# Attention values of a pair of heads in one group, and the end stage's loads spread out, in a two-layer hybrid decoder trunk on one Trainium2 core

## The chip, the core and the metric

The kernel runs on one core of a Trainium2 chip. The metric is the device time of one execution in microseconds (us), taken as the median of several. A profile of one further execution shows what each engine did: PE is the matmul engine (PEld its weight loads, which overlap with it), DVE the vector engine, ACT the scalar engine, POOL the general engine, and SP the queue that issues nearly all transfers. Each engine works through its own instructions in a fixed order; an instruction that has to wait holds up all that stand behind it on its engine.

## What is computed

Two layers over 512 tokens of width 1024. In each layer four branches read the same input; each result is gated, projected, and merged, and then an output projection, a residual and a layer norm follow. Branch B, causal attention with eight heads, is the one that changes here:

```python
def one_block(args):                       # one block of 128 queries, i = 0..3
    q_blk, i = args
    s = jnp.einsum('bqhd,bkhd->bhqk', q_blk, k).astype(jnp.float32) * scale
    s = jnp.where(key_idx[None, :] <= q_idx[:, None], s, MASK_VALUE)
    pr = jax.nn.softmax(s, axis=-1).astype(v.dtype)
    return jnp.einsum('bhqk,bkhd->bqhd', pr, v)
...
merged = jnp.sum(gates * proj, axis=2)     # over the four branches
out = merged @ w_out[l]
x = _layer_norm(DEEPNORM_ALPHA * x + out, ln_g[l], ln_b[l])
```

The other branches are a recurrent one (RWKV, 64x64 states), a convolution of width 31 with a layer norm, and a cross-attention into 256 memory tokens.

## The kernel before

**Who sets the order.** The kernel is written as many Python generators ("tasks") beside one stream of items. A planner (`Plan`, lines 67 to 196) keeps a modelled clock for each engine and, while the program is recorded, always steps the task that is due first; where no task is due, the stream goes on. The stream is the large projections: weights arrive through SP into two raw buffers (`weights`, line 430), are split into a high and a low part by ACT and DVE, and each product of 512 columns is made of three matmuls (`mm3`, line 461). What the planner decides is the fixed order in which each engine's instructions stand in the program; the chip does not reorder them. A task that yields "small" waits until other tasks of small matrices are due too (at most `GATHER` = 1500 ns of modelled time), so that matmuls that use half of the PE array stand together. The planner charges itself some time for each change between whole-array and half-array matmuls (`shape`, line 110).

**The attention branch.** The eight heads are taken as four pairs `hh`. For each pair `pair` (line 1460) takes one PSUM bank `mo` for the result and starts eight tasks `mla_block` (line 1477), for the query blocks i = 0 to 3 and the two heads h, at most three of them under way at a time. A block makes its scores `ms` on PE (128 queries by 128(i+1) keys, and the causal mask by one more matmul); DVE takes the maximum `nmm`; ACT the exponential `mP` with its sum; DVE divides; PE transposes the probabilities in pieces of 128x128 into `mt`; ACT copies them from PSUM to SBUF, `mPT` (lines 1502 to 1509). When the four blocks of i = 0, 1 are copied, six matmuls multiply them with the values `vtok` into `mo`; when the four of i = 2, 3 are, fourteen more follow (lines 1516 to 1520). These use 64 of the 128 columns of the array: one head goes to the upper half of `mo`'s partitions, the other to the lower. Each such float32 matmul shows as two records in the profile. After the second group `mo` is copied out (line 1526), and after the fourth pair the branch's pool is closed and the recurrent branch may begin.

The probabilities lie in a ring of four buffers with the tag `mPT`. A pair uses six of them: one for each head's blocks 0 and 1, and one each for blocks 2 and 3 of each head. So a copy reuses the buffer that was taken four before it, and must wait until the matmuls have read that.

**The merge.** `turn` (line 1537) decides when the gated result of a branch may be split into its high and low part (ACT and DVE, in `fin`, line 1548): when six of the eight merge steps of the branch ahead of it have been made. The order of the branches is cross-attention (3), attention (1), convolution (2), recurrent (0).

**The end stage.** When the recurrent branch is done, `start` (line 1641) opens a pool and issues the loads of the residual `z` in one go: eight of 128x512 in the first layer, sixteen of 128x256 in the second, and in the second also eight rows of layer-norm factors (`affine`, line 1651), four for the residual and four for the last norm. They go through SP's queue like the weights. A task `residual` then scales `z`, from the time when the last load it needs has landed by the planner's clock.

Of the kernel before, what the change touches and what calls it, by code (L numbers as in the profile page):

```python
# [265 lines left out]
def trunk_kernel(ctx: ExitStack, tc: tile.TileContext, A, out, dbg=None):  # L266
    nc = tc.nc
    plan = Plan(tc.keep_in_program_order)
    V, S, G = Engine(plan, nc.vector, "DVE"), Engine(plan, nc.scalar, "ACT"), Engine(plan, nc.gpsimd, "POOL")

    def MM(o, lhsT, rhs, start, stop, four=False):
        n = 1
        for d in rhs.shape[1:]:
            n *= d
        k, m = lhsT.shape[0], lhsT.shape[-1]
        plan.shape(64 if k <= 64 else 128, 64 if m <= 64 else 128)
        if max(k, m) <= 64:
            c = max(0.42 * n + 1.0, 29.0) if four else max(0.83 * n + 12.0, 59.0)
        elif rhs.dtype != F32 or n < 16:
            c = max(0.4167 * n + 13.0, 109.0) * (2 if rhs.dtype == F32 else 1)  # L280
        elif m <= 64:
            c = 0.83 * n + 3.0
        else:
            c = 1.667 * n + 5.0
        plan.op("PE", c, _names(o), _names(lhsT, rhs))
        plan.keep(nc.tensor.matmul(o, lhsT, rhs, start=start, stop=stop))  # L286
# [6 lines left out]
    def DMA(o, i, name=None):  # L293
        n = 512
        for d in o.shape[1:]:
            n *= d
        plan.dma(n, [name] if name else _names(o), _names(i))
        plan.keep(nc.sync.dma_start(o, i))
# [12 lines left out]
    pg = Space(plan, None, 0)  # L311
# [14 lines left out]
    def u(name, cols=512, dt=F32, p=128):  # L326
        return up.tile([p, cols], dt, tag="u", name=name)
# [217 lines left out]
    def close_phase():  # L545
        phase[0].close()
# [48 lines left out]
    def layer_items(l):  # L595
        items = []
        L = {}
        t_ = f"_{l}"
# [121 lines left out]
        def rwkv_unit(j0, hf, rkv):  # L720
# [485 lines left out]
        def xhead(h, q):  # L1206
# [3 lines left out]
            for tp in range(2):  # L1210
# [10 lines left out]
                yield  # L1221
            PT = []
            for mb in range(2):
# [31 lines left out]
        def m(name, cols, tag, bufs, p=128, dt=F32):  # L1255
            return L["mp"].tile([p, cols], dt, tag=tag, name=name, bufs=bufs)
# [101 lines left out]
        ymla = []  # L1358
# [101 lines left out]
        def pair(hh, qT, kT, there):  # L1460
            yield lambda: L["turn"] == hh and len(there) == 8
            mo, = yield from pg.take([128, 512], f"mo{hh}" + t_)
            plan.t = max(plan.t, *(plan.done[x][0] for x in there + [f"qTpe{hh}1" + t_]))
            yield
            left = [2]
            for i in range(4):
                if i % 2 == 0:
                    two, done = {}, []
                for h in range(2):
                    while L["jobs"] == 3:  # L1470
                        yield lambda: L["jobs"] < 3
                    L["jobs"] += 1
                    plan.spawn(mla_block(hh, h, i, (qT[h], kT[h]), mo, two, done, left))
                    yield
            L["turn"] += 1

        def mla_block(hh, h, i, T, mo, two, done, left):
# [24 lines left out]
            if i > 1:  # L1502
                PT = m("mPT" + q, 512, "mPT", 4)
            else:
                if h not in two:
                    two[h] = m("mPT" + q, 512, "mPT", 4)
                PT = two[h][:, 128 * i:]
            PT = two[h, i] = PT[:, 0:n]
            S.copy(PT, ps)
            pg.free()  # L1510
            L["jobs"] -= 1
            done.append(q)
            if len(done) < 4:
                return
            yield "small"
            for b in (i - i % 2, i - i % 2 + 1):
                for kb in range(b + 1):
                    for half in range(2):
                        MM(mo[HALF[half], 128 * b:128 * b + 128], vtok[kb][:, 128 * hh + 64 * half:128 * hh + 64 * half + 64],
                           two[half, b][:, 128 * kb:128 * kb + 128], start=kb == 0, stop=kb == b)  # L1520
            left[0] -= 1
            if left[0] == 0:
                L["pairs"] += 1
                yield
                yo = u(f"mo{hh}" + t_)
                S.copy(yo, mo)
                pg.free()
                ymla.append(yo)
                if len(ymla) == 4:
                    close_phase()  # L1530
                    L["mla"] = True


        merged = [None] * 8
        added = [0] * 4

        def turn(n):
            return n == 3 or added[{1: 3, 2: 1, 0: 2}[n]] >= 6

        def gate_items(n, base, name, ready, ys, res, op):  # L1540
            for i in range(4):
# [89 lines left out]
        E = {}  # L1631

        def end_items():
# [5 lines left out]
                return xs[zw * i // 512][:, zw * i % 512:zw * i % 512 + zw]  # L1639

            def start(get):
                yield lambda: "rwkv" in L
                E["ep"] = open_phase(f"ep{l}")
                ep = E["ep"]
                last = l + 1 == LAYERS
                E["z"] = [[ep.tile([128, zw], F32, tag=f"z{tb}{i}", name=f"z{tb}{i}" + t_) for i in range(zn)] for tb in range(4)]
                for tb in range(4):
                    for i in range(zn):
                        DMA(E["z"][tb][i], TOK[l][:, tb, zw * i:zw * i + zw])

                def affine(ll):
                    res = []
                    for n in ("ln_g", "ln_b"):
                        for i in range(2):
                            b = ep.tile([128, 512], F32, tag=f"{n}{i}{ll}", name=f"{n}{i}_{ll}" + t_)
                            DMA(b, A[n][ll, 512 * i:512 * i + 512].unsqueeze(0).to_broadcast([128, 512]))
                            res.append(b)
                    return res

                E["y"] = [0] * 4  # L1660
                if l:
                    ab = affine(l - 1)

                    def residual():
                        for i in range(zn):
                            for tb in range(4):
                                z, g, b = E["z"][tb][i], cut(ab[:2], i), cut(ab[2:], i)
                                if tb == 0:
                                    V.tensor_scalar(out=b, in0=b, scalar1=4.0 * ALPHA, scalar2=None, op0=ALU.mult)
                                V.scalar_tensor_tensor(out=z, in0=z, scalar=4.0 * ALPHA, in1=g, op0=ALU.mult, op1=ALU.mult)  # L1670
                                V.tensor_tensor(out=z, in0=z, in1=b, op=ALU.add)
                                E["y"][tb] += 1
                                yield "slack" if i else None
                    plan.spawn(residual(), plan.done[ab[3].tensor.name][0])
                else:
                    def residual():
                        for i in range(zn):
                            for tb in range(4):
                                z = E["z"][tb][i]
                                S.activation(z, z, AF.Copy, scale=4.0 * ALPHA)  # L1680
                                E["y"][tb] += 1
                                yield
                    plan.spawn(residual(), plan.done[E["z"][3][-1].tensor.name][0])
                if last:
                    E["ab"] = affine(l)

            def ahead(get):
                if l + 1 < LAYERS:
# [339 lines left out]
```

## Time and profile before

| | |
|---|---|
| three timed runs | 1508.65, 1511.56, 1513.46 us; median 1511.56 us |
| the profiled execution | 1509.62 us, of which the profile's span is 1507.8 us |
| PE busy | 1475.7 us, 98% of the span |
| DVE, ACT, POOL busy | 1072.6, 688.1, 134.3 us |
| granted TensorE clock, mean | 0.998 |
| attention branch on PE, first to last value matmul | 133.0 to 229.4 us in the first layer, 907.2 to 984.4 us in the second |
| end stage's loads issued by SP | 617.7 to 631.2 us in the first layer, 1377.9 to 1390.5 us in the second |

The profile has a page with busy times, a table of instruction groups and the chain of work that ended last; the trace behind it can be asked for the waits of each engine, for the instructions of a stretch in order of time (the timeline: start in us, duration in us, engine, line, operation, tiles written <- read, shape, count, and in brackets the idle time before it and what ended it), for one tile, and for busy times in windows of time. Buffer numbers are left out of tile names. Line 235 and 286 are helpers through which every instruction of an engine goes, so the tile names tell the stages apart. The end of a matmul is modelled; the distance between the starts of two is what PE needs for the first.

### The profile page before, as it was taken

The numbers are of one execution on the slowest core, as the hardware profiler recorded it, in microseconds if no ns is written. First come the engines' busy times: TensorE is split into PE (matmuls) and PEld (weight loads), VectorE is DVE, ScalarE is ACT, GpSimd is POOL, SyncE is SP. The second block draws the span as 40 slices with busy tenths as digits, with TensorE's granted clock in tenths as the row PEclk, the third lists the DMA queues.
The fourth block names the chain that finished last, engine by engine and source line by source line (L and its number), as shares of the span: only waits on it lengthen the run. The fifth ranks groups of instructions, "written<-read, shape, count | busy, mean of one in ns | idle before, by whom it ended". The sixth has DMA issues, their size and how long they took to land.

```text
span 1507.8 us, 29728 instructions
## 1 busy us (share of the span) xinstructions
PE 1475.7 (98%) x11896; PEld 1237.5 (82%) x11896; DVE 1072.6 (71%) x2231; ACT 688.1 (46%) x1507; POOL 134.3 (9%) x329
## 2 busy tenths in 40 slices
PE   8998999999999999999999999999999999999997
PEld 8887788888888888888999877888887888888886
DVE  5787998765758576555554889997866586757847
ACT  5544654345254454444255546533444354444432
POOL 0000000020403021000010000000030202020002
PEclk9999999999999999999999999999999999999999
DMA  6334333223232322433343242432232323234331
GB/s 212 119 115 98 105 100 98 96 77 95 62 86 81 95 88 81 140 98 120 121 144 114 83 126 68 121 109 93 82 98 69 94 74 94 65 104 142 126 119 63
DMA packets 89018, 153.54 MB, mean 102 GB/s; under 512 B 41008, under 2 KB 47152, under 8 KB 88880
## 3 DMA queue, kind: packets, MB, share of 16 engines
q1 hardware_dynamic: 88880, 151.65, 33.9%
q8 instruction: 93, 1.52, 0.4%
q14 instruction: 45, 0.37, 0.1%
HBM read 134.32 MB, written 5.77 MB: 93 GB/s over the span
## 4 chain that ended last, share of the span: by engine, by line
PE 91%; DVE 4%; DMA 2%; ACT 2%; issue 1%; SPq 0%; POOL 0%; ACTq 0%; DVEq 0%; POOLq 0%
PE ps_m L286 23%; PE po L286 12%; PE ps_xg L286 3%; PE ps_cg L286 3%; PE ps_rg L286 3%; PE ps_k L286 3%; PE ps_mg L286 3%; PE ps_v L286 3%; PE ps_r L286 3%; PE ps_val L286 3%; PE ms L286 2%; PE pz L286 2%; PE ps_glu L286 2%; PE ps_xq L286 2%; PE pl L286 2%; PE x L286 2%
## 5 line engine op out<-in xcount | busy, mean ns | idle before, releaser
L235 DVE SCALAR_TENSOR_TENSOR cacc<-hpad,prm,cacc 128x512 f32<-128x512 f32 x240 | 178.8, 747 | 3.3
L235 ACT ACTIVATE tm<-ps_m,prm 128x512 f32<-128x512 f32 x64 | 44.1, 689 | 141.2 <-PE ps_m L286 141.1
L235 DVE SCALAR_TENSOR_TENSOR mt<-tm,po 128x512 f32<-128x512 f32 x48 | 32.9, 686 | 71.2 <-PE po L286 69.0
L235 POOL TENSOR_TENSOR ZT<-ZT,tmpW 64x14 f32<-64x14 f32 (+6 forms) x112 | 42.7, 382 | 8.8
L235 ACT ACTIVATE mP<-ms,nmm 128x512 f32<-128x512 f32 (+3 forms) x64 | 33.7, 528 | 18.2 <-DVE nmm L235 17.4
L235 POOL TENSOR_TENSOR tmpW<-ZT,W 64x14 f32<-64x14 f32 (+6 forms) x112 | 39.3, 351 | 8.1
L235 POOL TENSOR_SCALAR ZT<-W 64x256 f32<-64x256 f32 x8 | 4.2, 524 | 383.8 <-DMA W<-scr 383.8
L235 ACT COPY mPT<-mt 128x512 f32<-128x512 f32 (+3 forms) x64 | 26.7, 428 | 22.2 <-PE mt L291 17.0
L235 DVE TENSOR_TENSOR merged<-merged,mt 128x512 f32<-128x512 f32 x48 | 33.5, 697 | 1.7
L235 POOL MEMSET D<- 128x8 f32 x8 | 1.1, 135 | 346.6 <-PE ms L286 327.1
L235 DVE TENSOR_REDUCE nmm<-ms 128x1 f32<-128x512 f32 (+3 forms) x64 | 29.9, 483 | 0.5
L291 PE MATMUL mt<-cst,mP 128*128 128x128 f32 x160 | 27.1, 277 | 2.4 <-DVE mP L235 2.3
L235 DVE TENSOR_SCALAR mP<-mP,smm 128x512 f32<-128x512 f32 (+3 forms) x64 | 24.8, 387 | 2.3
L235 DVE SCALAR_TENSOR_TENSOR merged<-tm,po 128x512 f32<-128x512 f32 x16 | 11.0, 687 | 20.8 <-PE po L286 19.1
L235 POOL TENSOR_SCALAR lrs<-lmv 128x1 f32<-128x1 f32 x8 | 2.5, 315 | 258.4 <-DVE lmv L235 256.7
L291 PEld LDWEIGHTS mt<-cst,mP 128*128 128x128 f32 x160 | 18.6, 141 | 8.0 <-ACT mo L235 2.2
L235 ACT ACTIVATE z<-z,lnb,lrs 128x256 f32<-128x256 f32 (+1 forms) x16 | 9.6, 648 | 31.1 <-DVE lnb L235 31.1
L235 ACT ACTIVATE yb<-yb,mr,gr 128x64 f32<-128x64 f32 x64 | 22.1, 428 | 2.7 <-DVE mr L235 2.7
L286 PE MATMUL ms<-kTl,qT 96*128 96x512 f32 (+3 forms) x64 | 22.3, 348 | 0.0
L286 PE MATMUL mo<-mPT,v 128*64 128x128 f32 x320 | 21.4, 278 | 0.5 <-ACT mPT L235 0.5
L235 POOL TENSOR_SCALAR gr<-gm 128x8 f32<-128x8 f32 x8 | 1.6, 198 | 215.5 <-DVE gm L235 215.5
L286 PEld LDWEIGHTS mo<-mPT,v 128*64 128x64 f32 x320 | 17.3, 136 | 4.0 <-issue 2.9
(3536 smaller groups left out, 5344.5 us busy)
## 6 DMA issues: line engine op xcount, KB each, us to landing
w<-in_w_ch_dram SPq DMA_DIRECT2D x146, 512.0 KB, 3.7
w<-in_w_o_dram SPq DMA_DIRECT2D x32, 512.0 KB, 3.7
w<-in_w_out_dram SPq DMA_DIRECT2D x16, 512.0 KB, 3.8
w<-in_w_lat_dram SPq DMA_DIRECT2D x16, 336.0 KB, 3.2
w<-in_w_mk_dram SPq DMA_DIRECT2D x8, 512.0 KB, 3.5
w<-in_w_mv_dram SPq DMA_DIRECT2D x8, 512.0 KB, 3.4
w<-in_w_qk_dram SPq DMA_DIRECT2D x8, 320.0 KB, 3.1
x<-in_xT_dram SPq DMA_DIRECT2D x8, 256.0 KB, 5.7
```

The lines of the kernel that those rows point to most:

```text
L235: return self.plan.keep(f(*a, **k))
L286: plan.keep(nc.tensor.matmul(o, lhsT, rhs, start=start, stop=stop))
L291: plan.keep(nc.tensor.transpose(o, i, ident))
```

## The change

1. All eight blocks of a pair are multiplied with the values in one group of twenty matmuls, when the last is copied (`len(done) < 8`); `left` goes.
2. The ring of four buffers goes. Each head has two buffers of 384 columns for its blocks 0 and 1 (tag `mPT0`, `mPT1`), and one of 896 columns for its blocks 2 and 3 (`mPW0`, `mPW1`). Before a pair takes these, the planner waits until the group of the pair before it (for the wide ones), or of two pairs before it (for the narrow ones), has been recorded.
3. `turn` asks for eight merge steps of the branch ahead in place of six.
4. `start` only starts a task `opening`, which issues the end stage's loads step by step: 3 us of planner time after the loads of each 128 tokens, 2 us after each row of factors.

```diff
-            left = [2]
+            two, done = {}, []
             for i in range(4):
-                if i % 2 == 0:
-                    two, done = {}, []
                 for h in range(2):
...
-            if i > 1:
-                PT = m("mPT" + q, 512, "mPT", 4)
-            else:
-                if h not in two:
-                    two[h] = m("mPT" + q, 512, "mPT", 4)
-                PT = two[h][:, 128 * i:]
-            PT = two[h, i] = PT[:, 0:n]
-            S.copy(PT, ps)
+            if (h, i // 2) not in two:
+                if L["pairs"] < hh - 1 + i // 2:
+                    yield lambda: L["pairs"] >= hh - 1 + i // 2
+                two[h, i // 2] = m("mPT" + q, 896, f"mPW{h}", 1) if i > 1 else m("mPT" + q, 384, f"mPT{h}", 2)
+            e = (0, 128, 0, 384)[i]
+            S.copy(two[h, i // 2][:, e:e + n], ps)
             pg.free()
             L["jobs"] -= 1
             done.append(q)
-            if len(done) < 4:
+            if len(done) < 8:
                 return
             yield "small"
-            for b in (i - i % 2, i - i % 2 + 1):
+            for b in range(4):
                 for kb in range(b + 1):
                     for half in range(2):
+                        e = (0, 128, 0, 384)[b] + 128 * kb
                         MM(mo[HALF[half], 128 * b:128 * b + 128], vtok[kb][:, 128 * hh + 64 * half:128 * hh + 64 * half + 64],
-                           two[half, b][:, 128 * kb:128 * kb + 128], start=kb == 0, stop=kb == b)
-            left[0] -= 1
-            if left[0] == 0:
-                L["pairs"] += 1
...
+                           two[half, b // 2][:, e:e + 128], start=kb == 0, stop=kb == b)
+            L["pairs"] += 1
...
         def turn(n):
-            return n == 3 or added[{1: 3, 2: 1, 0: 2}[n]] >= 6
+            return n == 3 or added[{1: 3, 2: 1, 0: 2}[n]] >= 8
...
             def start(get):
+                plan.spawn(opening())
+                yield
+
+            def opening():
                 yield lambda: "rwkv" in L
...
                     for i in range(zn):
                         DMA(E["z"][tb][i], TOK[l][:, tb, zw * i:zw * i + zw])
+                    plan.t += 3000.0
+                    yield
...
                             DMA(b, A[n][ll, 512 * i:512 * i + 512].unsqueeze(0).to_broadcast([128, 512]))
                             res.append(b)
+                            plan.t += 2000.0
+                            yield
                     return res
...
                 if l:
-                    ab = affine(l - 1)
+                    ab = yield from affine(l - 1)
...
                 if last:
-                    E["ab"] = affine(l)
+                    E["ab"] = yield from affine(l)
```

More of the change, by code (lines that the diff above doesn't have):

```diff
@@ L1472, in pair, with mla_block @@
                     L["jobs"] += 1
-                    plan.spawn(mla_block(hh, h, i, (qT[h], kT[h]), mo, two, done, left))
+                    plan.spawn(mla_block(hh, h, i, (qT[h], kT[h]), mo, two, done))
                     yield
             L["turn"] += 1
-        def mla_block(hh, h, i, T, mo, two, done, left):
+        def mla_block(hh, h, i, T, mo, two, done):
             n = 128 * i + 128
@@ L1512, in mla_block @@
             done.append(q)
-            if len(done) < 4:
+            if len(done) < 8:
                 return
             yield "small"
-            for b in (i - i % 2, i - i % 2 + 1):
+            for b in range(4):
                 for kb in range(b + 1):
                     for half in range(2):
+                        e = (0, 128, 0, 384)[b] + 128 * kb
                         MM(mo[HALF[half], 128 * b:128 * b + 128], vtok[kb][:, 128 * hh + 64 * half:128 * hh + 64 * half + 64],
-                           two[half, b][:, 128 * kb:128 * kb + 128], start=kb == 0, stop=kb == b)
-            left[0] -= 1
-            if left[0] == 0:
-                L["pairs"] += 1
[L1524 to L1531, printed above, removed]
+                           two[half, b // 2][:, e:e + 128], start=kb == 0, stop=kb == b)
+            L["pairs"] += 1
+            yield
+            yo = u(f"mo{hh}" + t_)
+            S.copy(yo, mo)
+            pg.free()
+            ymla.append(yo)
+            if len(ymla) == 4:
+                close_phase()
+                L["mla"] = True
         merged = [None] * 8
@@ L1657, in affine @@
                             res.append(b)
+                            plan.t += 2000.0
+                            yield
                     return res
```

## The prediction

> **What bounds the kernel now.** I read the page first, then PE's waits, then the timelines of ACT and PE around the attention branch.
>
> ```profile
> span 1507.8 us, 29728 instructions
> PE 1475.7 (98%) x11896; PEld 1237.5 (82%) x11896; DVE 1072.6 (71%) x2231; ACT 688.1 (46%) x1507; POOL 134.3 (9%) x329
> PE 91%; DVE 4%; DMA 2%; ACT 2%; issue 1%; SPq 0%; POOL 0%; ACTq 0%; DVEq 0%; POOLq 0%
> ```
>
> The third line is the chain that ended last, by engine. PE works for 1475.7 of 1507.8 us and carries 91% of the chain. So only two things can move the time much: the matmul work itself, with what PE loses at changes of shape, and the 32.1 us in which PE stands still. The first place to look at those is PE's own waits (total us, times, longest):
>
> ```profile
> PE pl L286 <- DVE w0l L235: 6.2, 1, 6.2
> PE pq L286 <- DVE xql L235: 2.4, 1, 2.4
> PE mt L291 <- DVE mP L235: 2.3, 2, 1.8
> PE ps_xq L286 <- DVE xql L235: 1.5, 3, 1.0
> PE zw L286 <- issue: 1.2, 1, 1.2
> ```
>
> The first is the start of the program, the second (before 110 us) lies ahead of all that changes. Of the rest only the waits of `mt` belong to the code that changes. What makes DVE late there? The timeline of ACT shows it:
>
> ```profile
> 140.90 0.21 ACT L235 ACTIVATION_READ_ACCUMULATOR mP<-ms,nmm 128x1 f32 x1
> 145.01 0.59 ACT L235 COPY mPT<-mt 128x512 f32<-128x512 f32 x1 [3.91 <-PE mo L286]
> ...
> 917.25 0.27 ACT L235 COPY mPT<-mt 128x128 f32<-128x128 f32 x1 [1.34 <-PE mo L286]
> ```
>
> And PE in the first of these two places:
>
> ```profile
> 140.60 0.60 PE L291 MATMUL mt<-cst,mP 128*128 128x128 f32 x4
> ...
> 144.11 1.09 PE L286 MATMUL mo<-mPT,v 128*64 128x128 f32 x14
> 145.65 1.09 PE L286 MATMUL mo<-mPT,v 128*64 128x128 f32 x14 [0.46 <-ACT mPT L235]
> ...
> 147.62 0.40 PE L286 MATMUL ps_val<-xh,w27l 128*128 128x512 f32 x1
> 149.82 0.41 PE L291 MATMUL mt<-cst,mP 128*128 128x128 f32 x2 [1.80 <-DVE mP L235]
> ```
>
> The copy of a block of four transposes wants the ring buffer that block 2 of the same pair holds. The matmuls that read that buffer stand in the second value group, and this very copy feeds that group. So ACT stands for 3.91 us until PE has come to the group, PE then stops in the middle of the group for 0.46 us until the copy is made, and everything queued behind the copy on ACT, above all the exponentials of the next blocks, is late, so that PE waits another 1.80 us for a `mt`. The second place, 1.34 us of ACT, costs PE nothing that I can find.
>
> **The change, part by part.** The built order of the changed kernel has the same 11896 matmul records; only their order differs.
>
> *Fewer changes between whole and half array.* PE's rows around a value group, around another, and after a short run of half-array matmuls of the recurrent branch:
>
> ```profile
> 132.96 0.88 PE L286 MATMUL mo<-mPT,v 128*64 128x128 f32 x12
> 133.76 0.55 PE L291 MATMUL mt<-cst,mP 128*128 128x128 f32 x3
> ...
> 165.33 0.40 PE L286 MATMUL ps_xq<-xh,w29h 128*128 128x512 f32 x1
> 165.56 0.40 PE L286 MATMUL ps_xq<-xh,w29l 128*128 128x512 f32 x1
> 165.89 1.75 PE L286 MATMUL mo<-mPT,v 128*64 128x128 f32 x28
> 167.57 0.66 PE L291 MATMUL xt<-cst,xP 128*128 128x128 f32 x4
> ...
> 602.67 0.45 PE L286 MATMUL w<-S,Gs 64*64 64x64 f32 x8
> 603.05 0.50 PE L286 MATMUL ps_m<-xl,w92h 128*128 128x512 f32 x1
> 603.39 0.39 PE L286 MATMUL ps_m<-xh,w92h 128*128 128x512 f32 x1
> ```
>
> From start to start, 28 records take 1.68 us and 12 take 0.80, so 16 more take 0.88: 0.055 each. What is left of either, 1.68 - 28 x 0.055 = 0.14, is paid once per group. The large matmul ahead of a group takes 0.33 (165.56 to 165.89) in place of 0.23, 0.10 more; the one behind a run takes 0.34 (603.05 to 603.39), 0.11 more. A run of half-array matmuls thus costs about 0.10 + 0.14 + 0.11 = 0.35 us beyond its matmuls. The built order has 8 value runs in place of 16, but 59 runs of the recurrent branch in place of 57 (both new ones in the second layer, where the planner happened to put them apart). The latter have the same loss at the exit; I take the same price. Net 8 - 2 = 6 runs, **-2.1 us**. This is PE work on a path that is nearly all PE, so it counts in full.
>
> *The ring's waits go.* Going through the built order of before with the ring of four, I find exactly two copies whose transposes stand on PE ahead of the matmuls that free their buffer; they are the two of the ACT rows above. In the changed order there is none: a copy into a wide buffer belongs to transposes that stand behind the previous pair's group on PE in all twelve cases, by at least 5.7 us of PE work (twenty-five large matmuls of 0.23). So the ACT wait of 3.91 us goes, and with it PE's 0.46 and 1.80: **-2.3 us**. What is late next? The same blocks' chains through DVE and ACT still have to fit between the scores and the transposes on PE. For the four blocks that stand behind the stuck copy the changed order puts more PE work there than before (the tightest has 3.6 us in place of 2.9); I count no new stall, and price one in rival A.
>
> *The group waits for all eight copies.* In the changed order PE has between the last transposes of a pair and its group mostly six large matmuls, 6 x 0.23 = 1.4 us (1.2 at the least, 2.6 at the most). The copy takes 0.59 (the row at 145.01), and the block copied last is read only in the last part of the group. That leaves over 0.8 us for a queue on ACT. I take nothing, and keep up to 1 us for the upper end of the range. The copies themselves are as many and as wide as before.
>
> *`turn` at eight.* The split of the next branch's results begins two merge steps later. What hides it (timeline, chain, and the tile view of `mo` with min/median/max in ns):
>
> ```profile
> 376.81 0.39 PE L286 MATMUL po<-yxg3h,w58l 128*128 128x512 f32 x1
> ```
>
> ```profile
> 397.61 5.46 PE po L286 x24
> ```
>
> ```profile
> L235 ACT CAST ymg3h<-mo x2: 611/616/621, 392.8 to 1122.4; 128x512 fp32r<-128x512 f32 x2
> L235 DVE TENSOR_TENSOR ymg3l<-mo,ymg3h x2: 682/684/685, 395.3 to 1124.0; 128x512 fp32r<-128x512 f32 x2
> ```
>
> From the eighth merge step of branch 3 to the first of branch 1, 397.6 - 377.0 = 20.6 us pass, filled with gate projections. Four splits take 4 x (0.62 + 0.68) = 5.2 us if nothing overlaps. Uncovered, the six hand-overs (three in each layer) would cost up to 31 us; the changed order leaves over 20 us of PE work in each, and I count nothing.
>
> *The loads.* SP's burst in the second layer, and PE in the two windows around it (busy us of PE, PEld, DVE, ACT, POOL, clock, DMA share, GB/s):
>
> ```profile
> 1377.88 7.45 SPq L298 DMA_DIRECT2D z<-xtok  x16
> ...
> 1390.63 0.49 SPq L298 DMA_DIRECT2D w<-in_w_o_dram  x1
> ```
>
> ```profile
> 1350.00:1400.00 50.00, 49.44 (x601) 39.98 (x591) 34.69 (x107) 19.74 (x44) 3.68 (x4) 1.00 0.42 137
> 1400.00:1450.00 50.00, 50.00 (x223) 41.38 (x222) 35.98 (x66) 19.73 (x35) 0.00 (x0) 1.00 0.34 113
> ```
>
> The weight block behind the burst is issued nearly 13 us after it began, yet PE is full through 1400 to 1450: weights ahead cover it. In the changed order that block goes ahead of the burst, and two more go between its loads; the residual's last factor comes behind three weight blocks that it was ahead of, up to some 20 us later. The scaled residual is first needed when the output projection adds to it, in the last stage, and DVE (busy 36 of 50 us in the second window) has room to make it later. Both sides hide: **0**, at most 1 us either way through weights that come sooner or later.
>
> **The sum.** -2.1 - 2.3 = -4.4 us. It is made against the profiled execution (1509.6 us, span 1507.8 and 1.8 around it), which gives 1505.2. The median of the timed runs is 1.9 us above that execution, so I forecast **1507.2 us** as their like, 0.29% below 1511.56.
>
> **The rivals.** About 0.3%, 4.5 us, is what a measurement of this kernel can tell from no change; the forecast lies just inside.
>
> *A: only the runs count.* ACT is set free, but the freed blocks find DVE or a PSUM bank late, and PE stands about as long elsewhere. For it: the three waits before `ps_xq` show that other chains through DVE are nearly late too. Against it: the late `mt` follows from the stuck copy alone, since PE, ACT and DVE all stood behind it. Time: 1511.6 - 2.1 = 1509.5.
>
> *B: more idle time goes.* The freed ACT and DVE also clear the next wait, 1.0 us before `ps_xq` in the row above, and the reordered second layer loses the 1.2 us of `zw`, for which the profile names no releaser. Time: 1507.2 - 2.2 = 1505.0.
>
> *C, slower: the merged group is late.* ACT works in order, and where a queue stands before the last copy, PE waits at the group, eight times. It decides at about 0.8 us of queue ahead of the copy beyond its own 0.59. This row speaks for it: the copy of transposes that began at 149.82 and took 0.41.
>
> ```profile
> 150.82 0.40 ACT L235 COPY mPT<-mt 128x256 f32<-128x256 f32 x1
> ```
>
> It began 0.59 us after their end, behind casts of weights; that is inside the margin. To undo the gain, each group must lose 4.4 / 8 = 0.55 us on average. With a queue of 2.0 us each would lose 1.2: 1507.2 + 9.6 = 1516.8.
>
> [...]
>
> ```profile
> 10.53 0.48 PE L286 MATMUL pl_0x<-w0l,xh 128*128 128x336 f32 x1
> 10.80 0.48 PE L286 MATMUL pl_0x<-w0h,xh 128*128 128x336 f32 x1
> ...
> 13.19 0.32 PE L286 MATMUL pl_0x<-w1l,xh 128*128 128x336 f32 x1
> 13.34 0.32 PE L286 MATMUL pl_0x<-w1h,xh 128*128 128x336 f32 x1
> ```
>
> The same matmul takes 0.27 us at 10.5 and 0.15 at 13.2: some 22 of them, 2.7 us in all, were slow after the 6.2 us of idle start. [...]
>
> *D: the loads matter.* If the burst of 13 us did delay weights unseen, the spread gains at most the 0.6 us that PE idles in the window 1350 to 1400: 1506.6.
>
> **How the numbers follow.** Forecast 45%, of which not quite half falls below 1507.0 by the spread of runs (1508.65 to 1513.46 before); A 20%, nearly all within 0.3%; B 20%, nearly all faster; C 11%, most of it slower; D 4%, half faster. Faster by over 0.3%: 0.20 + 0.20 + 0.02 + 0.02 = 0.44; slower 0.09; within 0.47. The range takes in A and B with 2 us of scatter at either side, and leaves out C's upper part: 1502.6 to 1511.8.
>
> **What would show it.** Right: eight value runs of 40 records, 2.33 us each (40 x 0.055 + 0.14); no ACT wait on PE `mo` before a copy; `mt` without its 1.8 us; PE's busy time some 2 us lower, its idle time some 2 us lower. Wrong: PE waits on ACT `mPT` at the groups (C), or idle time equal to before with new names (A), or waits on weights after 1380 (D with the other sign).

## The result, and the profile after

The changed kernel takes 1505.82 us in the median of 7 runs (1504.20 to 1506.48), the kernel before 1511.56 (1508.65 to 1513.46). The ratio is 0.9968, with a 95% interval of 0.9959 to 0.9978: 4.8 us less, between 3.3 and 6.2. The profiled execution took 1505.99 us, 0.8 over the 1505.2 that the sum gave for it.

The page of the changed kernel: the span, the busy times and the chain by engine.

```profile
span 1504.2 us, 29727 instructions
...
PE 1475.6 (98%) x11896; PEld 1238.4 (82%) x11896; DVE 1072.9 (71%) x2231; ACT 689.1 (46%) x1507; POOL 135.9 (9%) x329
...
PE 86%; DVE 6%; DMA 3%; ACT 2%; POOL 1%; issue 1%; SPq 1%; ACTq 0%; POOLq 0%; DVEq 0%
```

PE's busy time is not the announced 2 us lower in this execution (1475.7 before). But its granted clock was 0.93 and 0.73 in the windows of 5 us from 105 and 110 us, ahead of all that changed, which takes 0.35 + 1.35 = 1.7 us; in the trace of before it was 1.00 there. Two later profiles with the same order on PE and without that loss (e8_after_noloads and e9_after_again) have 1474.4 and 1474.2, so 1.3 to 1.5 us less. PE's share of the chain is 86% in place of 91%; it is 87% in a version below (e10_split_again) that takes as long, so that this share tells little of the time. PE's waits (total us, times, longest) show the idle time that did go:

```profile
PE pl L286 <- DVE w0l L235: 5.9, 1, 5.9
PE pq L286 <- DVE xql L235: 1.9, 1, 1.9
...
PE mt L291 <- DVE mP L235: 1.2, 2, 0.8
PE ps_xq L286 <- DVE xql L235: 1.0, 2, 0.8
PE x L286 <- DVE PT L235: 0.7, 1, 0.7
...
PE gb_0x L286 <- issue: 0.6, 1, 0.6
...
PE zw L286 <- DVE yc L235: 0.3, 1, 0.3
```

The start of the program (`pl`) and the wait before `pq` lie ahead of the change. The wait of 1.8 before `mt` is gone (two of at most 0.8 have that name now), and so are the 1.2 before `zw`; waits of 0.7 before `x` and 0.6 before `gb_0x` are new. At the place where ACT had stood for 3.91 us, its timeline now reads:

```profile
141.12 0.75 ACT L235 COPY mPT<-mt 128x512 f32<-128x512 f32 x2
142.64 0.47 ACT L235 ACTIVATE mP<-ms,nmm 128x256 f32<-128x256 f32 x1 [0.77 <-DVE nmm L235]
```

and PE's, with the first merged group:

```profile
141.69 0.23 PE L286 MATMUL ms<-causal,idb 128*128 128x128 bf16 x1
...
143.29 2.40 PE L286 MATMUL mo<-mPT,v 128*64 128x128 f32 x40
145.62 0.38 PE L286 MATMUL ms<-kTl,qT 96*128 96x256 f32 x1
```

No copy waits for a value group any more. From 143.29 to 145.62 the 40 records take 2.33 us, as forecast, without a gap; all eight groups take 2.33 to 2.34.

To see where the time went I cut both traces at matmuls that every order has in the same place: the first `mt` of a layer, its first `ps_wlal` (the attention branch lies between), the first `g` and the first `pz` (the recurrent branch and the gate projections). The windows of the kernel before (first layer's attention and recurrent stretch, then the second layer's; length, busy us of PE, PEld, DVE, ACT, POOL, granted clock, DMA share, GB/s):

```profile
126.49:257.65 131.16, 127.82 (x785) 104.36 (x785) 116.51 (x257) 72.06 (x187) 0.30 (x1) 1.00 0.32 88
313.14:708.89 395.75, 395.32 (x3969) 325.30 (x3969) 248.56 (x526) 173.09 (x362) 59.43 (x143) 1.00 0.32 95
899.39:1028.05 128.66, 128.57 (x763) 104.36 (x761) 117.23 (x236) 66.61 (x165) 0.12 (x1) 1.00 0.34 96
1083.54:1453.62 370.08, 367.99 (x3850) 302.84 (x3849) 250.88 (x548) 158.80 (x340) 54.91 (x143) 1.00 0.33 97
```

and of the changed kernel:

```profile
126.29:253.97 127.68, 126.47 (x785) 104.44 (x786) 115.58 (x255) 71.09 (x186) 0.14 (x1) 1.00 0.31 89
309.46:705.43 395.97, 395.31 (x3969) 325.26 (x3969) 249.65 (x528) 173.07 (x362) 59.86 (x143) 1.00 0.32 95
895.11:1023.26 128.15, 127.72 (x762) 104.51 (x761) 114.24 (x232) 66.76 (x165) 0.12 (x1) 1.00 0.34 96
1078.76:1449.98 371.22, 369.49 (x3850) 303.07 (x3849) 253.91 (x552) 159.93 (x341) 56.28 (x143) 1.00 0.33 97
```

The first layer's attention is 3.48 us shorter: idle time (length less PE busy) fell from 3.34 to 1.21, PE's work by 1.35. The second layer's is 0.51 shorter. The second layer's recurrent stretch, which nobody touched, is 1.14 us longer, and 1.5 of that is PE's work. The stretches not listed differ by 0.8 us at the most, and the first layer's end stage and the second's from `pz` on, which the loads serve, by 0.01.

### The profile page after: what moved, and what is told of

The parts are those of the page before. It is cut to its first block, busy times and chain, and to the rows that moved or that the text cites. A ratio compares the mean times of both kernels' runs of the same rounds, so it can differ in the third digit from the quotient of the medians.

```text
span 1504.2 us, 29727 instructions
## 1 busy us (share of the span) xinstructions
PE 1475.6 (98%) x11896; PEld 1238.4 (82%) x11896; DVE 1072.9 (71%) x2231; ACT 689.1 (46%) x1507; POOL 135.9 (9%) x329
## 3 DMA queue, kind: packets, MB, share of 16 engines
q8 instruction: 93, 1.52, 0.4%
## 4 chain that ended last, share of the span: by engine, by line
PE 86%; DVE 6%; DMA 3%; ACT 2%; POOL 1%; issue 1%; SPq 1%; ACTq 0%; POOLq 0%; DVEq 0%
PE ps_m L286 23%; PE po L286 11%; PE ps_cg L286 3%; PE ps_rg L286 3%; PE ps_xg L286 3%; PE ps_v L286 3%; PE ps_k L286 3%; PE ps_val L286 3%; PE pz L286 2%; PE ps_glu L286 2%; PE ps_mg L286 2%; PE ps_r L286 2%; PE pl L286 2%; PE ps_xq L286 2%; DMA w<-in_w_ch_dram 2%; PE ms L286 2%
## 5 line engine op out<-in xcount | busy, mean ns | idle before, releaser
L235 ACT ACTIVATE mP<-ms,nmm 128x128 f32<-128x128 f32 (+3 forms) x64 | 33.7, 528 | 28.1 <-DVE nmm L235 25.5
L235 ACT COPY mPT<-mt 128x128 f32<-128x128 f32 (+3 forms) x64 | 26.6, 426 | 12.9 <-PE mt L291 12.6
L235 DVE TENSOR_REDUCE nmm<-ms 128x1 f32<-128x128 f32 (+3 forms) x64 | 30.5, 485 | 0.2
L235 DVE TENSOR_SCALAR mP<-mP,smm 128x128 f32<-128x128 f32 (+3 forms) x64 | 24.8, 387 | 2.3
L286 PE MATMUL ms<-kTl,qT 96*128 96x128 f32 (+3 forms) x64 | 22.6, 354 | 0.4 <-ACT w157h L235 0.3
L235 ACT ACTIVATE xP<-xs,nmx 128x256 f32<-128x256 f32 x32 | 15.2, 475 | 12.1 <-DVE nmx L235 11.5
L286 PE MATMUL ms<-kTh,qT 96*128 96x128 f32 (+3 forms) x64 | 20.6, 322 | 0.0
```

The costliest lines, as they stand in the source:

```text
L235: return self.plan.keep(f(*a, **k))
```

## The experiments

My theory: the gain is the ring's wait (2 us of idle time) and the merged runs (2.2 us of work by the two attention stretches), less what two more runs in the second layer's recurrent stretch take; loads and `turn` give nothing. The rivals: only the runs count (A), the loads or the later `turn` carry it, or the difference is scatter. The ratios are each to runs of the kernel before on the same chip.

| label | what runs | runs of half-array matmuls | ratio to before (95%) | median us |
|---|---|---|---|---|
| e1_loads | before, loads spread | 73 | 1.0000 (0.9991 to 1.0009) | 1510.00 |
| e2_turn | before, `turn` at 8 | 73 | 1.0005 (0.9994 to 1.0016) | 1510.03 |
| e3_ring6 | before, ring of six | 73 | 0.9981 (0.9970 to 0.9992) | 1507.76 |
| e4_split | after, two groups | 73 | 0.9972 (0.9962 to 0.9982) | 1506.24 |
| e5_quarter | after, four groups | 90 | 1.0016 (1.0007 to 1.0025) | 1512.43 |
| e6_after_d0 | after, no planned time between loads, nor behind the copies of the keys | 65 | 0.9980 (0.9971 to 0.9988) | 1507.09 |
| e7_after_63 | as e6_after_d0, gathering time 2000 | 63 | 0.9964 (0.9951 to 0.9976) | 1505.14 |
| e8_after_noloads | after, loads in a burst | 67 | 0.9968 (0.9955 to 0.9980) | 1504.84 |
| e9_after_again | after | 67 | 0.9971 (0.9960 to 0.9981) | 1506.40 |
| e10_split_again | as e4_split | 73 | 0.9971 (0.9960 to 0.9981) | 1506.18 |
| e11_after_65 | as e6_after_d0, but planned time between `z` loads | 65 | 0.9932 (0.9919 to 0.9946) | 1500.65 |
| e12_after_63 | as e11_after_65, gathering time 1600 | 63 | 0.9953 (0.9940 to 0.9965) | 1503.58 |

**One part alone.** e1_loads takes the kernel before with the new `start` and `opening` of the diff.

> The kernel before with one edit: the end stage's loads are spread over time, as in the changed kernel; the value groups, their buffers and the merge condition stay as before. Mine: nothing, 1511.6 us within 1 us, and ACT's 3.91 us wait on PE mo with PE's 0.46 and 1.80 us of idle are still there. The rival that the loads carry the gain: 3 to 5 us less, with less PE idle in the last 150 us.

e2_turn changes one number of the kernel before.

```diff
-            return n == 3 or added[{1: 3, 2: 1, 0: 2}[n]] >= 6
+            return n == 3 or added[{1: 3, 2: 1, 0: 2}[n]] >= 8
```

> The kernel before with one edit: the split of the next branch's results waits for eight merge steps in place of six. Mine: nothing, within 1 us of the kernel before, the splits covered by 20 us of gate projections. The rival that the later split moves work to a better place: 1 to 3 us less. The rival that it costs: PE waits for the split results after the last gate projections, up to 5 us for each of six hand-overs.

Both give nothing by the timed runs, and in both traces PE still waits 1.8 us before the same `mt`. The rivals that one of them carries the gain fall.

e3_ring6 has the kernel before's two `m("mPT" + q, 512, "mPT", 4)` with six buffers:

```diff
-                PT = m("mPT" + q, 512, "mPT", 4)
+                PT = m("mPT" + q, 512, "mPT", 6)
```

> The kernel before with one edit: the ring of the copied transposes has six buffers in place of four, so that in the built order no copy wants a buffer whose reader stands behind it on PE. The order on PE and the number of runs of half-array matmuls (73) stay as before. Mine: 2.1 us less, all of it idle time in the first layer's attention (3.34 us there before, 1.2 then), and that stretch's PE work as before (127.8 us). Rival A (only the runs count): within 0.5 us of before, the idle time is back under other names. If the ring carried the whole gain: 4.8 us less.

It is 0.19% faster (2.9 us, between 1.2 and 4.5). The windows of its first layer's attention and its second layer's recurrent stretch:

```profile
126.26:255.28 129.02, 127.59 (x786) 104.28 (x785) 116.45 (x257) 72.04 (x186) 0.22 (x1) 1.00 0.32 89
...
1082.37:1452.60 370.23, 368.18 (x3849) 303.23 (x3849) 250.75 (x548) 158.81 (x341) 55.24 (x143) 1.00 0.33 97
```

Against the rows of before, 2.14 us are gone where I had them, 1.91 of it idle time (3.34 to 1.43). The rest of the kernel is as it was, but for the stretch ahead of the second layer's attention, which is 1.44 us longer: there the granted clock was 0.70 and 0.95 in the windows of 5 us from 890 and 895 us, 1.75 us in all, and 1.00 in the trace of before. The freed time does not come back as waits, so rival A falls.

**The merging undone, and doubled the other way.** e4_split is the changed kernel with two groups per pair; e10_split_again is the same kernel once more, beside e9_after_again, the changed kernel itself, on one chip.

```diff
-            two, done = {}, []
+            two, left = {}, [2]
             for i in range(4):
+                if i % 2 == 0:
+                    done = []
...
-            if len(done) < 8:
+            if len(done) < 4:
                 return
             yield "small"
-            for b in range(4):
+            for b in (i - i % 2, i - i % 2 + 1):
...
+            left[0] -= 1
+            if left[0]:
+                return
             L["pairs"] += 1
```

> The changed kernel with one part undone: the values of a pair are again taken in two groups (two query blocks each), 73 runs of half-array matmuls in place of 67, with the wide buffers, the spread loads and the merge condition of the changed kernel kept. The two runs that the changed order adds to the second layer's recurrent branch are gone as well. Mine: 2 us slower than the changed kernel in the two attention stretches (2.2 us of work by its trace), 1.1 us faster in the second layer's recurrent stretch, so about 1 us slower than the changed kernel and 3 to 4 us faster than before. The rival that merging carries the whole gain: as slow as before. Rival A (only the runs count) gives the same, as slow as before.

> The changed kernel as it is, on the same chip as the three that follow. Both theories: 0.32% faster than before, within 0.1%.

> The version with values in two groups per pair, buffers and loads of the changed kernel (73 runs of half-array matmuls), beside the changed kernel on one chip. Mine: merging earns 1.3 us in the two attention stretches (by the traces so far) and loses 1.5 to 2 in the second layer's recurrent stretch, where the changed order has two more runs: this version equal to the changed kernel within 1 us. The rival that the merged groups are worth the 2.1 us of my prediction net: 2 us slower than the changed kernel.

Both are 0.29% faster than before, and the means of their runs differ by 0.1 us, with an uncertainty of about 1.5: in this order the step that gives the change its name earns nothing that can be measured. The windows show why. The changed kernel, first and second layer's attention and the second layer's recurrent stretch (e9_after_again):

```profile
126.05:253.69 127.64, 126.44 (x784) 104.56 (x785) 115.58 (x255) 71.11 (x186) 0.14 (x1) 1.00 0.30 89
...
896.39:1023.62 127.23, 127.19 (x762) 104.54 (x761) 114.34 (x232) 66.81 (x165) 0.12 (x1) 1.00 0.34 97
1079.12:1450.64 371.52, 369.54 (x3850) 303.50 (x3849) 253.56 (x552) 159.79 (x341) 55.35 (x143) 1.00 0.33 97
```

and the version with two groups (e10_split_again):

```profile
126.74:255.28 128.54, 127.25 (x784) 104.33 (x785) 116.48 (x257) 72.28 (x187) 0.22 (x1) 1.00 0.32 89
...
898.65:1027.27 128.62, 128.53 (x762) 104.45 (x761) 117.21 (x236) 66.51 (x165) 0.12 (x1) 1.00 0.34 96
1082.76:1451.94 369.18, 367.78 (x3849) 303.45 (x3849) 251.32 (x548) 159.30 (x340) 55.36 (x143) 1.00 0.33 97
```

Merging saves 0.90 and 1.39 us in the two attention stretches, 2.3 in all, and the order that the planner then finds costs 2.34 in the recurrent stretch, 1.76 of it work and the rest idle time. The sum is nil. The other pair of profiles, the first of the changed kernel and e4_split, gives 1.1 us saved and 2.05 lost in the same stretches, so each of these sizes is good to about 1 us.

e5_quarter cuts the groups of e4_split once more:

```diff
-            for b in (i - i % 2, i - i % 2 + 1):
+            for b in (i,):
```

with `left` at 4 and `len(done) < 2`.

> The kernel with values in two groups per pair, cut once more: one group for each query block, four per pair, buffers and everything else kept. 90 runs of half-array matmuls in place of its 73. By the price of my prediction (0.35 us a run) 17 more runs make it 6 us slower than the version with two groups; by the price that the attention stretches of the traces so far give (1.3 us for eight runs, 0.17 each) 2.9 us slower, so about 1509 us where the kernel before takes 1510. The rival that runs cost next to nothing and the ring is all: within 1 us of the version with two groups.

It is 0.44% slower than the version with two groups (1.0016 against 0.9972), 6.6 us for 17 more runs: 0.39 each, with an uncertainty of about 0.12 by the two intervals. The pages say the same without timing: in windows of 5 us the granted clock falls short of 1.00 by 3.4 us in all in either execution up to 1495 us, so their busy times can be compared. Page of e5_quarter, then of e10_split_again:

```profile
span 1511.4 us, 29715 instructions
...
PE 1483.0 (98%) x11896; PEld 1239.3 (82%) x11896; DVE 1072.4 (71%) x2231; ACT 687.8 (46%) x1507; POOL 134.0 (9%) x329
```

```profile
span 1506.2 us, 29715 instructions
...
PE 1477.2 (98%) x11896; PEld 1240.7 (82%) x11896; DVE 1072.6 (71%) x2231; ACT 688.9 (46%) x1507; POOL 135.7 (9%) x329
```

PE works 5.8 us more for 17 runs: 0.34 each. This is the price with all that comes along, since the order of the rest moved too (the first layer's attention stretch became 4.3 us shorter, its recurrent stretch 7.6 longer). The price of my prediction, 0.35, stands; the expectation of 0.17 that I had taken from e4_split's stretches meanwhile does not, nor does the rival that runs cost nothing.

**The loads and the number of runs.** e8_after_noloads is the changed kernel with the old `start`.

> The changed kernel with one part undone: the end stage's loads are again issued in one burst. 67 runs of half-array matmuls, as in the changed kernel. Mine: the same as the changed kernel within 1 us, 0.32% faster than before. The rival that the loads matter once the rest is changed: 1 to 3 us slower than the changed kernel.

It equals the changed kernel. In e6_after_d0 the loads yield, but add no planned time. Its edit, and that of the three versions below, also takes away the 2 us of planned time behind each of the four copies of the rotated keys at the start of each layer, which the expectations do not name:

```diff
                 for x, y in zip(kT, kr):
                     DMA(x[64:96].bitcast(F32), y.bitcast(F32))
-                plan.t += 2000.0
+                plan.t += 0.0
...
-                    plan.t += 3000.0
+                    plan.t += 0.0
...
-                            plan.t += 2000.0
+                            plan.t += 0.0
```

> The changed kernel with one edit: the spread loads yield to the planner but add no planned time, which gives a built order with 65 runs of half-array matmuls in place of 67; the two that are gone are the two in the second layer's recurrent branch that the change added. Mine: the 1.1 us that this stretch lost against the kernel before comes back, so 1 to 2 us faster than the changed kernel, 0.40% faster than before. The rival that this stretch's loss is scatter of the execution and not the runs: the same as the changed kernel, 0.32%.

Here I was wrong: it has two runs fewer, and is no faster than the changed kernel. By the medians it is 2.2 us slower than e8_after_noloads on the same chip, though the intervals of their ratios overlap. PE's longest wait from 1380 to 1460, and its windows (columns as above; the last is the second layer's recurrent stretch) in e6_after_d0:

```profile
PE ps_m L286 <- ACT w221h L235: 2.7, 1, 2.7
```

```profile
1395.00:1400.00 5.00, 2.25 (x9) 1.61 (x8) 4.48 (x9) 2.34 (x5) 0.00 (x0) 0.94 0.62 250
1400.00:1405.00 5.00, 4.79 (x12) 3.23 (x11) 4.90 (x12) 0.98 (x2) 0.00 (x0) 0.50 0.24 57
1405.00:1410.00 5.00, 5.00 (x21) 4.05 (x20) 2.74 (x9) 1.24 (x3) 0.00 (x0) 0.88 0.44 155
```

```profile
1076.63:1452.02 375.39, 371.80 (x3850) 305.10 (x3849) 250.22 (x547) 159.57 (x340) 53.62 (x143) 0.99 0.32 96
```

A weight block comes late, and around and behind the wait the granted clock is 0.94, 0.50 and 0.88: 0.3 + 2.5 + 0.6 = 3.4 us more are lost than the 2.7 of the wait. SP's timeline shows the cause: the block is issued behind the whole burst.

```profile
1377.63 8.76 SPq L298 DMA_DIRECT2D z<-xtok  x16
...
1389.28 1.41 SPq L298 DMA_DIRECT2D ln_b<-in_ln_b_dram  x2
1390.78 0.63 SPq L298 DMA_DIRECT2D w<-in_w_ch_dram  x1
```

By the view of the transfers the block lands 7.0 us after its issue, at about 1397.8. ACT's cast of it, at 1398.81, stands behind another that waits for DVE until 1398.28, so about 1 us of the 2.7 is ACT's order (an estimate from these times).

e11_after_65 is e6_after_d0 with the 3 us between the loads of `z` put back, so against the changed kernel it drops the planned time behind the copies of the keys and between the vectors. e7_after_63 and e12_after_63 are e6_after_d0 and e11_after_65 with another gathering time:

```diff
-GATHER = 1500.0
+GATHER = 1600.0
```

(2000.0 in e7_after_63.)

> The changed kernel, where only the loads of the scale and shift vectors add no planned time; the loads of the branch results stay spread. 65 runs of half-array matmuls: the two that the change added to the second layer's recurrent branch are gone, and weights go between the loads again. Mine: without the 2.75 us wait for weights near 1396 us and the lower clock behind it that the version without any planned time showed (together some 6 us in its last-but-one stretch), so 1 to 2.5 us faster than the changed kernel. The rival that the weights come late as soon as the vectors are loaded in one go: 1 to 2 us slower than the changed kernel, as before.

> The changed kernel, its spread loads adding no planned time and the planner's gathering time at 2000 in place of 1500: 63 runs of half-array matmuls in place of 67 (two fewer in each layer's recurrent branch). Mine: another 0.5 to 1 us off the version with 65, 2 to 3 us faster than the changed kernel, 0.45 to 0.5% faster than before. The rival that the waits of the gathered matmuls come back as idle time: no faster than the changed kernel.

> As the version with 65 runs, and the planner's gathering time at 1600 in place of 1500: 63 runs, two fewer in the first layer's recurrent branch. Mine: another 0.7 us off, 2 to 3 us faster than the changed kernel, 0.45 to 0.5% faster than before. The rival that gathering only trades runs for waits: the same as the version with 65.

SP's timeline in e11_after_65 has the weights between the loads again, the block in question 11 us earlier, and the wait is gone:

```profile
1377.81 1.99 SPq L298 DMA_DIRECT2D z<-xtok  x4
1379.89 0.38 SPq L298 DMA_DIRECT2D w<-in_w_ch_dram  x1
1380.32 5.18 SPq L298 DMA_DIRECT2D z<-xtok  x8
```

The planned time between the loads of `z` is all that separates the two: 0.9980 against 0.9932, and 375.39 against 367.94 us (row below) in the second layer's recurrent stretch. So the spread of the loads, worth nothing in the changed kernel, is worth some 7 us in this order. It need not be: e7_after_63 has the burst too, in yet another order, and no such wait.

At 0.9932 it is the fastest kernel of this study, by the medians 9.4 us ahead of the kernel before and 5.8 ahead of the changed kernel on the same chip, more than the 1 to 2.5 I expected. Its second layer, attention and recurrent stretch:

```profile
890.10:1022.26 132.16, 131.44 (x783) 107.85 (x783) 120.91 (x242) 67.34 (x168) 0.12 (x1) 1.00 0.34 97
...
1077.76:1445.70 367.94, 367.65 (x3850) 303.33 (x3849) 249.58 (x547) 159.74 (x340) 55.48 (x143) 1.00 0.33 98
```

The recurrent stretch takes 367.94 in place of 371.52 us: 1.9 less of work with its 28 runs in place of 30, and 1.7 less of idle time (1.98 to 0.29). Another 1.1 goes in the second layer's attention and what lies ahead of it together (the first `mt` stands at another place in this order, so the two are taken as one), where the waits before `xo` (2.7 us in e9_after_again) have gone; the first layer is as long. None of this comes from the loads of the vectors. In e11_after_65 SP issues the first of them at 1388.0 us, and from 1381.0 us on (1386.0 in e9_after_again) PE has the same order in both kernels and takes the same 118.9 us to the end. What differs earlier can only come from the planned time behind the copies of the keys. SP's timelines show it, e9_after_again first:

```profile
45.03 0.53 SPq L298 DMA_DIRECT2D kTl<-krl  x1
45.65 0.53 SPq L298 DMA_DIRECT2D w<-in_w_ch_dram  x1
```

```profile
48.61 0.59 SPq L298 DMA_DIRECT2D kTl<-krl  x1
49.24 0.58 SPq L298 DMA_DIRECT2D w<-in_w_ch_dram  x1
```

With the planned time a weight block goes between the copies, without it behind all of them, and PE's order differs from there on. This costs PE 1.8 us at once (the wait before `ps_val` near 51 us is 3.0 in place of 1.2), and the new order wins it back and more. How much of the gain is the two runs and how much the luck of a new order isn't told apart, and the line of the keys alone was not run.

With two runs fewer still (e12_after_63) it is slower again, 0.9953. The first layer's recurrent stretch shows 1.7 us of it, with 1.52 us idle:

```profile
304.99:704.87 399.88, 398.36 (x3982) 328.34 (x3981) 251.31 (x531) 173.01 (x363) 61.19 (x143) 1.00 0.33 96
```

In e11_after_65 the same stretch is 398.20 long with 0.18 idle, and with 398.02 of work no more of that. There the gathered matmuls traded runs for waits, as the rival said, and at a loss; e7_after_63, with 0.9964, is no faster than the changed kernel either.

Merging with `turn` left at six was not tried: in that order engines wait for each other in a circle.

## Why the prediction was right in the sum and wrong in a term

*The total.* Forecast: 1507.2 and 0.29% less; measured: 1505.82, 0.32% less (0.22 to 0.41), and 0.29% in the repeat. The forecast was in the interval, though not by its own terms. The two profiled executions are 3.6 us apart, the medians 5.7, the ratio says 4.8: single executions of one kernel scatter by several us (1508.65 to 1513.46 for the kernel before; the last section shows what goes with it), and the 1.9 us that I added to come to the median of before were such scatter.

*The ring's waits, -2.3 us.* Right. The ring of six alone takes 2.14 us out of the first layer's attention, and 2.9 (1.2 to 4.5) by the timed runs. Chain and place were as described: the stuck copy, PE's stop inside the group, the late `mt`. This is the part of the change that pays.

*The runs, -2.1 us.* This is the step that failed: "Net 8 - 2 = 6 runs, -2.1 us". Merging alone nets nothing (0.9971 with and without it). The price of a run was right (0.34 to 0.39 by e5_quarter). Against the kernel before, PE's work in e9_after_again is 1.38 us lower in each layer's attention, together the 2.8 of eight runs; against the version with two groups it is 2.3 us of time, and 1.1 by the other pair of profiles. What was mis-sized is the other side, "both new ones in the second layer", priced at 0.7: that stretch has 1.55 us more work than before, and takes 2.34 us longer than in the same kernel with two groups. So the net in work is -1.2 in place of -2.1 against the kernel before, and in time nothing against the version with two groups. The price by itself still holds for the shortest of these runs (timeline of the changed kernel, second layer):

```profile
1271.59 0.40 PE L286 MATMUL ps_m<-xh,w202l 128*128 128x512 f32 x1
1271.92 0.45 PE L286 MATMUL w<-S,Gs 64*64 64x64 f32 x8
1272.30 0.50 PE L286 MATMUL ps_m<-xl,w202h 128*128 128x512 f32 x1
1272.64 0.40 PE L286 MATMUL ps_m<-xh,w202h 128*128 128x512 f32 x1
```

Alone, eight `w` take 0.38 from start to start; as part of a run of 72 (64 `x` and 8 `w`, 1.31 to 1.33 against 1.09 for 64 `x` alone) they take 0.22 to 0.24: 0.15 more. The matmul behind is 0.11 longer than its 0.23, the one ahead 0.10: 0.36. Two of these are 0.7. Of the 1.76 us of work, about 1 us remains that I can't give to single matmuls; it is bound to this order, since e9_after_again, e8_after_noloads and the first profile have 369.5 us of work there and the profiles above of orders with 28 runs have 367.7 to 368.2 (e6_after_d0, which lost clock there, apart). The remaining 0.6 is idle time, which I had not priced at all: the waits in this stretch stand elsewhere (0.7 before `x`, 0.6 before `gb_0x`); that they come from the runs torn apart is not shown.

*What made up for it.* The version with two groups is already at 0.9971, 0.1% below the ring of six (0.9981), without merging. By the windows it is 0.5 us shorter in the first layer's attention and 1.05 in the recurrent stretch; the wait of 1.2 before `zw` is gone there and one of 0.7 before `ps_v` has come. This is the part of rival B that came true, about 1 us; by the timed runs alone the intervals of the two overlap. It was not separated further into wide buffers, loads and `turn`.

*The merged group's own wait, 0.* Right. No group waits for a copy, so rival C did not occur.

*`turn`, 0, and the loads, 0.* Right, each alone (e1_loads, e2_turn) and the loads inside the changed kernel (e8_after_noloads), so rival D did not occur. But e6_after_d0 shows that the burst is not hidden by nature: there a weight block issued behind it cost 2.7 us of wait and 3.4 of clock. In the kernel before, and in the changed one with the burst, PE has no wait for weights at this place.

*The clock, 0.* The sum has no term for a loss of granted clock inside the kernel. In the trace of before there was none (1.00 in every window of 5 us up to 1500 us); in other executions there was, 1.7 us at a time, as the last section shows. What slowed the first matmuls of the program, some 22, (0.27 us each in place of 0.15) is not shown: the granted clock reads 1.00 there too.

## What to carry to other kernels

Cut a change into its parts on the chip before believing its name: here a larger ring alone brought more than half of the gain (2.9 of 4.8 us, both uncertain by over 1), and the merging nothing in the order that came of it. Where a planner sets the order, a local saving is paid for or doubled by the new order elsewhere; compare the stretches that weren't touched, and try a few harmless settings of the planner: here the planned time behind a few copies of keys, dropped beside the setting that was meant, gained more than the whole change. So read an edit line by line before giving its effect a cause. A count of runs is a good price list but no forecast of the waits: 65 runs beat 67 in one version and not in another, and 63 lost to 65.

## What the hardware showed beside

In these profiles a wait of PE of some 2 us was often followed by a lower granted clock, and then cost more than its length. In e1_loads, around the wait of 1.81 us before `mt` that the ring causes:

```profile
145.00:150.00 5.00, 3.13 (x26) 2.47 (x23) 4.67 (x10) 3.01 (x11) 0.00 (x0) 0.91 0.00 0
150.00:155.00 5.00, 5.00 (x30) 3.77 (x30) 4.93 (x14) 3.56 (x11) 0.00 (x0) 0.75 0.42 123
```

The granted clock falls behind the wait and takes 0.45 + 1.25 = 1.7 us; in the traces of before and e2_turn, with the same wait, it doesn't (1.00 in the same windows). Over the fourteen profiles a pattern shows: the wait before `pq` near 107 us was followed by such a drop (0.66 to 0.82 in the lowest window of 5 us) in six of the seven executions where it lasted 1.9 us or more (not in the kernel before, at 2.4 us), in none where it was shorter; the wait before `ps_val` near 51 us in all four where it lasted 2.2 to 3.0 us (0.66 to 0.75), in none of the ten where it lasted 1.0 to 1.2. Near 890 us, where two waits of 0.5 to 1.4 and 1.5 to 1.6 us lie 2 us apart, it came in six of eight executions (0.70 in e3_ring6, 0.71 in e10_split_again, 0.72 in e5_quarter), and in neither of the two with the second wait alone. Why waits of one length are followed by a drop in one execution and not in another is not shown. The usual loss is 1.7 us. In the changed kernel the granted clock is 0.67, 0.50, 0.50 and 0.63 in the windows of 1 us from 109 us, together 1.7 us, that of 3.4 us at 0.50; a matmul that took 0.23 us from start to start takes 0.43 there. Two such losses came behind the 2.7 us in e6_after_d0 (0.50 through the whole window of 5 us from 1400). The scatter of one kernel's executions goes with the clock: of the 15 runs of the kernel before beside e9_after_again, the three longest (1512.5 to 1513.6 us) have a mean granted clock of 0.993 to 0.995, the three shortest (1507.9 to 1509.1) 0.996 to 0.998. The ring's wait thus cost more than its 2.1 us in some executions, which fits the 2.9 by the timed runs but is not proven by it.
